# A macaron encoder layer on one core: four matmuls on a cleared tile first, the first squares on VectorE, wide operand copies, loads by SyncE alone

## The chip, the cores and the metric

The kernel runs on one core of one Trainium2 chip. The metric is device time of one execution in microseconds. Before the change three runs gave 1293.13, 1294.99 and 1297.63 us, median 1294.99.

Engines go by the names of the profile: PE is TensorE (PEld its weight loads), DVE is VectorE, ACT is ScalarE, POOL is GpSimd, SP is SyncE, which here only issues transfers.

## The reference

One layer on 512 tokens of width 1024, all in float32:

```python
x = x + 0.5 * swiglu(rmsnorm(x, ffn1_norm), ffn1_w1, ffn1_w3, ffn1_w2)
h = rmsnorm(x, mix_norm)
x = x + hybrid_mixer(h, w_in, ...)      # dilated window attention | GQA | gates
x = x + 0.5 * swiglu(rmsnorm(x, ffn2_norm), ffn2_w1, ffn2_w3, ffn2_w2)
return rmsnorm(x, final_norm)

def rmsnorm(x, g):
    return x * lax.rsqrt(jnp.mean(x * x, axis=-1, keepdims=True) + EPS) * g
def swiglu(x, w1, w3, w2):
    return (jax.nn.silu(x @ w1) * (x @ w3)) @ w2
```

The feed-forward width is 2816, so w1 and w3 are each 22 chunks of 128 features. Only the opening of the first feed-forward part, and the start of the second, matter below.

## The kernel before

**Layout.** x lies transposed in eight tiles x0 to x7 of 128 features by 512 tokens. Every matmul of weights is done in three: each operand is split into a high part (H, a cast by ACT) and a low remainder (L, a subtraction by DVE), and H·H, L·H and H·L are added in PSUM (`mm3`, lines 223 to 225). So a block of 128 features needs hH and hL of each x tile (`norm_h`: x times the norm's gain) and wh and wl of the weights (`prep`, lines 208 and 209).

**The norm's factor is applied after the products.** They are made with x times gain; the factor per token, r = (mean of squares + eps)^-0.5, is multiplied into the result (`done1`, line 441: t = mm x R). It is made beside the first matmuls. `squares` lets ACT square each x tile, and `norm_sq` adds them into acc: on POOL for x1 to x5, on DVE for x6 and x7. `stat_r` sums acc over features with small matmuls (stat, line 383); DVE makes ms (line 375), POOL raises it to -0.5 (r, line 376). `stat_R` lets PE transpose r into all partitions (rb, line 391), and ACT copies that to R (line 393).

**The first feed-forward part** begins with four plain feature pairs. The first pair (`pair`) runs both its chunks side by side, tile by tile, as x and the weights land: 16 steps, numbered 0 to 15, each with three matmuls. Then six single chunks (`feat`) of eight steps follow. A table of hooks names the step behind which something is put into PE's order: squares at 12, stat_r at 23, stat_R at 27. PE's order is as written; the other engines' orders are set by a planner when the program is built, each engine then runs its own list strictly in that order.

From the fifth feature pair on the chunks are done by a Strassen scheme. It needs sums and differences of halves of the scaled x (TH, TL). `t_steps` prepares them in 15 steps of ACT and DVE, every second step from 12 on: `put` copies x times gain into raw tiles T (line 313), `sub` and `neg` form the combinations (lines 326, 327), `part` splits them (lines 318, 319). The second feed-forward part does the same from step 1 on, at every step.

**Buffers and queues.** Weights land in three buffers wr of 512 KB each; three pairs of wh and wl take their split forms, so a cast waits until PE is done with the chunk three before. The Strassen weights come in wa and wt: SP loads wt (line 189), then POOL issues a transfer that adds a second matrix onto it (line 190); DVE adds wt and wa into ws (line 207). Four PSUM banks hold products: a fifth chunk starts when the first product is multiplied by R. x tiles 1 and 3 are issued by ACT's queue, all others and the weights by SP's.

Of the kernel before, what the change touches and what calls it, by code (L numbers as in the profile page):

```python
# [11 lines left out]
F32 = mybir.dt.float32  # L12
# [18 lines left out]
GAP_B = 1  # L31
LAG = 1
LAST = 2
T = 512
D = 1024
NK = 8
# [32 lines left out]
class Layer:  # L69
    def __init__(self, ctx, tc, a):  # L70
        self.tc, self.nc, self.a = tc, tc.nc, a
        ctx.enter_context(tc.manual_schedule(engines={mybir.EngineType.PE}))
        pool = lambda n, **k: ctx.enter_context(tc.tile_pool(name=n, **k))
        self.dram = pool("dram", bufs=1, space=DRAM)
        self.cst = pool("cst", bufs=1)
        self.wb = pool("wb", bufs=1)
        self.tmp = pool("tmp", bufs=4)
        self.psm = pool("psm", bufs=4, space=PSUM)
        self.psa = pool("psa", bufs=4, space=PSUM)
        nc = self.nc  # L80
        c = self.cst
        self.x = [c.tile([128, T], F32, name=f"x{d}") for d in range(NK)]
        self.par = c.tile([128, 48], F32, name="par")
        nc.scalar.dma_start(self.par, a["par"])
        self.ident = c.tile([128, 128], F32, name="ident")
        self.ones = c.tile([128, 1], F32, name="ones")
        nc.vector.memset(self.ones, 1.0)
        self.mhalf = c.tile([128, 4], F32, name="mhalf")
        nc.vector.memset(self.mhalf, -0.5)
        nc.scalar.activation(self.ones, self.ones, AF.Copy)  # L90
        self.r = c.tile([128, 8], F32, name="r")
        self.R = c.tile([128, T], F32, name="R")
        self.acc = c.tile([128, T], F32, name="acc")
        self.open_h()
        self.gate_d = self.dram.tile([16, 128, T], F32, name="gate_d")
        self.qk_d = self.dram.tile([2 * NSQ, 128, T], F32, name="qk_d")
        self.items = ([("v", 0), ("v", 1), ("sw", 0), ("v", 2)] + [("g", j) for j in range(2)]
                      + [("qk", f) for f in range(NSQ, 12)] + [("g", j) for j in range(2, 9)]
                      + [("b", g) for g in range(3)] + [("g", j) for j in range(9, 16)])
        span = {"v": ("wav", 4), "qk": ("waq", 2), "g": ("wg", 1), "b": ("wb", 4)}  # L100
        self.order = self.ffn_order("a")
        for kind, n in self.items:
            if kind == "sw":
                self.order += [("swq", at) for at in self.slots(range(0, NSQ, 2))]
                continue
            name, m = span[kind]
            self.order += [(name, m * n + i) for i in range(m)]
        self.order += [("wab", i) for i in range(12)] + [("wo", i) for i in range(8)]
        self.order += self.ffn_order("b")
        self.raws, self.tiles, self.used, self.wx, self.TQ = {}, [], 0, None, None  # L110
        self.rings = {k: [] for k in BUFS}
        self.index = {it[:2]: n for n, it in enumerate(self.order)}
        self.kind = [self.home(it) for it in self.order]
        self.todo = sorted((n for n, t in enumerate(self.kind) if t != "ws"), key=lambda n: n - EARLY * (self.kind[n] == "wt"))
# [187 lines left out]

    def t_steps(self, g, gp):
        nc = self.nc
        raw = []
        flat = lambda t, c: t[:, c].rearrange("p k n -> p (k n)")

        def put(d):
            if d == 0:
                both = [gp.tile([128, 2048], F32, tag=f"g{2 + c}", name=f"T{c}") for c in range(2)]  # L310
                raw.extend(both[c // 2][:, 1024 * (c % 2):1024 * (c % 2) + 1024] for c in range(4))
            for half in range(2):
                nc.scalar.activation(raw[(0 if d < 4 else 2) + half][:, 256 * (d % 4):256 * (d % 4) + 256],
                                     self.x[d][:, 256 * half:256 * half + 256], AF.Copy, scale=self.par[:, g + d:g + d + 1])

        def part(c):
            src, H, L = raw[c], flat(self.TH, max(0, c - 1)), flat(self.TL, max(0, c - 1))
            nc.scalar.copy(H, src)
            nc.vector.tensor_sub(L, src, f32(H))

        def part1(k):
            src, H, L = raw[1][:, 256 * k:256 * k + 256], self.hH[k][:, 256:512], self.hL[k][:, 256:512]
            nc.scalar.copy(H, src)
            nc.vector.tensor_sub(L, src, f32(H))

        sub = lambda o, a, b: nc.vector.tensor_sub(raw[o], raw[a], raw[b])
        neg = lambda o, a, b: nc.vector.scalar_tensor_tensor(raw[o], raw[a], -1.0, raw[b], op0=ALU.mult, op1=ALU.subtract)
        return ([lambda d=d: put(d) for d in range(NK)]
                + [lambda: sub(0, 0, 1), lambda: sub(1, 3, 1), lambda: neg(3, 3, 0), lambda: part(0),
                   lambda: neg(2, 3, 2), lambda: part(3), lambda: part(2)], [lambda k=k: part1(k) for k in range(4)])  # L330
# [27 lines left out]
        nc.scalar.activation(self.hH[d], self.x[d], AF.Copy, scale=gc)  # L358
        nc.vector.scalar_tensor_tensor(self.hL[d], self.x[d], gc, f32(self.hH[d]), op0=ALU.mult, op1=ALU.subtract)

    def norm_sq(self, d):
        nc = self.nc
        if d == 0:
            nc.scalar.activation(self.acc, self.x[d], AF.Square)
        else:
            sq = self.tmp.tile([128, T], F32, tag="t", name="sq")
            nc.scalar.activation(sq, self.x[d], AF.Square)
            eng = nc.vector if d >= NK - 2 else nc.gpsimd
            eng.tensor_add(self.acc, self.acc, sq)

    def rpow(self, dst, src, inv):
# [713 lines left out]
    def layer(self, out):  # L1085
        nc, tc = self.nc, self.tc
        for n in range(2):
            self.raws[n] = self.ring("wr", self.todo.pop(0), 0, n)
            self.tiles.append(self.ring("wh", n, 0, n))
        for d in (1, 3):  # L1090
            nc.scalar.dma_start(self.x[d], self.a["x"][d])
        for d in range(NK):
            if d not in (1, 3):
                nc.sync.dma_start(self.x[d], self.a["x"][d])
            if d % 2 == 0:
                s = slice(128 * d, 128 * d + 256)
                for c in range(2):
                    nc.sync.dma_start(self.raws[c][:, s], self.a["w13a"][c][:, s])
            self.norm_h(d, G_FFN1)
            if d % 2 == 0:  # L1100
                for raw, (H, L) in zip(self.raws.values(), self.tiles):
                    nc.scalar.copy(H[:, s], raw[:, s])  # L1102
                    nc.vector.tensor_sub(L[:, s], raw[:, s], f32(H)[:, s])
        nc.sync.dma_start(self.ident, self.a["ident"])

        def squares():
            for d in range(NK):
                self.norm_sq(d)

        with tc.tile_pool(name="bt", bufs=1, side="right") as bp:  # L1110
            hooks = {12: squares, 23: self.stat_r, 27: self.stat_R, "T": (12, 2)}
            self.bias_open(bp)
            side = {(0, d): lambda g=d: self.bias_rows(g) for d in range(3)}
            for h in range(8):
# [101 lines left out]
```

## Time and profile before

| what | us |
|---|---|
| median of three runs | 1294.99 |
| the profiled execution | 1294.96 |
| its span, first to last instruction | 1293.2 |
| PE busy | 1269.7 |
| first matmul | 5.89 |
| longest idle time of PE behind the first matmul | 3.47, at the transposes rb |
| ACT, DVE, POOL busy | 589.5, 880.8, 125.9 |

Times in the profile count from the span's start. A timeline row gives start, duration, engine, source line, operation, output<-input and shape, and in brackets the idle time of that engine just before with what ended it; several equal instructions in a row are merged with their count. Matmuls overlap, so the step between two starts is what one costs. The granted clock of the whole execution is 0.994 of full speed.

### The profile page before, as it was taken

Reading aid. Unit: us, or ns where it says so; the run is one execution under the profiler, and the core shown is the slowest. Engines: PE = TensorE matmul, PEld = TensorE weight load, DVE = VectorE, ACT = ScalarE, POOL = GpSimd, SP = SyncE. Lnnn points to the kernel's source line nnn. Section 1 sums busy time; section 2 is a strip of 40 time slices with the busy share of each in tenths; the row PEclk is TensorE's granted clock in tenths of the full one; section 3 lists DMA queues with packets and bytes.
Section 4 is the critical chain, followed back from the end, with each engine's and each line's share of the span. In section 5 each row is a group of like instructions: output and inputs, shape, how many; then the busy total and the mean of one; then the engine's idle time right before and its main releaser. Section 6 shows DMA issues by size and latency. Waiting matters only on the chain.

```text
span 1293.2 us, 19954 instructions
## 1 busy us (share of the span) xinstructions
PE 1269.7 (98%) x7994; PEld 1124.1 (87%) x7994; DVE 880.8 (68%) x1334; ACT 589.5 (46%) x883; POOL 125.9 (10%) x128
## 2 busy tenths in 40 slices
PE   7999999999999999999999999999999999999997
PEld 5897899899889999877888878888889989988996
DVE  5775578558783687576657898655577847774775
ACT  7552355235463443545324455543475415442553
POOL 3111011010110112100001100000301000100001
PEclk9999999999999999999999999999999999999998
DMA  8664776351373774743232221345627636753322
GB/s 255 195 175 155 205 179 175 131 135 48 123 205 122 205 196 155 246 108 92 98 112 81 75 74 41 106 151 165 214 83 193 182 94 175 170 165 98 99 82 66
DMA packets 85549, 181.91 MB, mean 141 GB/s; under 512 B 12480, under 2 KB 19024, under 8 KB 85456
## 3 DMA queue, kind: packets, MB, share of 16 engines
q1 hardware_dynamic: 67616, 140.22, 32.5%
q0 software_dynamic: 16832, 39.34, 15.1%
q8 instruction: 63, 1.03, 0.3%
q10 hardware_dynamic: 1008, 1.07, 0.2%
q14 instruction: 30, 0.25, 0.1%
HBM read 168.98 MB, written 15.29 MB: 142 GB/s over the span
## 4 chain that ended last, share of the span: by engine, by line
PE 87%; DVE 4%; DMA 4%; issue 3%; POOL 1%; ACT 1%; SPq 0%; POOLq 0%; DVEq 0%
PE mm L223 23%; PE mm L225 22%; PE mm L224 22%; PE Y L223 3%; PE Y L224 3%; PE Y L225 3%; DMA wt<-in_waq 2%; PE X L223 2%; PE X L225 2%; PE X L224 1%; PE S L776 1%; DVE wl L209 1%; PE mm L827 1%; PE Tb L966 1%; PE T L845 1%
## 5 line engine op out<-in xcount | busy, mean ns | idle before, releaser
L208 ACT CAST wh<-wr 128x1024 fp32r<-128x1024 f32 x142 | 148.8, 1049 | 216.1 <-PE mm L224 137.9
L209 DVE TENSOR_TENSOR wl<-wr,wh 128x1024 fp32r<-128x1024 f32 x142 | 173.5, 1223 | 58.4 <-ACT wh L208 58.0
L223 PE MATMUL mm<-hH,wh 128*128 128x256 f32 (+1 forms) x600 | 201.9, 336 | 5.9 <-ACT wh L1102 5.9
L225 PE MATMUL mm<-hH,wl 128*128 128x256 f32 (+1 forms) x600 | 198.1, 330 | 0.0
L224 PE MATMUL mm<-hL,wh 128*128 128x256 f32 (+1 forms) x600 | 197.7, 330 | 0.0
L223 PE MATMUL mm<-gg,wh 128*128 128x512 f32 (+1 forms) x376 | 143.1, 380 | 0.0
L225 PE MATMUL mm<-gg,wl 128*128 128x512 f32 (+1 forms) x376 | 142.6, 379 | 0.0
L224 PE MATMUL mm<-gg,wh 128*128 128x512 f32 (+1 forms) x376 | 142.5, 379 | 0.0
L223 PEld LDWEIGHTS mm<-hH,wh 128*128 128x128 f32 x600 | 114.1, 190 | 19.8 <-ACT wh L1102 5.9
L225 PEld LDWEIGHTS mm<-hH,wl 128*128 128x128 f32 x600 | 113.8, 190 | 11.4 <-DVE wl L209 0.3
L224 PEld LDWEIGHTS mm<-hL,wh 128*128 128x128 f32 x600 | 113.8, 190 | 9.9
L208 ACT CAST wh<-wa 128x1024 fp32r<-128x1024 f32 x48 | 50.4, 1051 | 101.0 <-PE mm L224 49.4
L490 DVE TENSOR_TENSOR u<-mm,R 128x512 f32<-128x512 f32 (+1 forms) x52 | 33.8, 650 | 85.1 <-PE mm L225 84.9
L223 PE MATMUL mm<-TH,wh 128*128 128x256 f32 x304 | 84.8, 279 | 1.6 <-DVE c L462 1.6
L225 PE MATMUL mm<-TH,wl 128*128 128x256 f32 x304 | 84.7, 279 | 0.0
L224 PE MATMUL mm<-TL,wh 128*128 128x256 f32 x304 | 84.7, 278 | 0.0
L223 PEld LDWEIGHTS mm<-gg,wh 128*128 128x128 f32 x376 | 70.8, 188 | 15.2 <-issue 1.1
L225 PEld LDWEIGHTS mm<-gg,wl 128*128 128x128 f32 x376 | 70.8, 188 | 14.1
L224 PEld LDWEIGHTS mm<-gg,wh 128*128 128x128 f32 x376 | 70.9, 188 | 13.9
L208 ACT CAST wh<-ws 128x1024 fp32r<-128x1024 f32 x48 | 50.4, 1051 | 69.2 <-PE mm L224 51.3
L209 DVE TENSOR_TENSOR wl<-wt,wh 128x1024 fp32r<-128x1024 f32 x48 | 58.7, 1223 | 33.1 <-ACT wh L208 32.8
L208 ACT CAST wh<-wt 128x1024 fp32r<-128x1024 f32 x48 | 50.3, 1050 | 67.0 <-PE mm L224 37.2
(230 smaller groups left out, 3182.6 us busy)
## 6 DMA issues: line engine op xcount, KB each, us to landing
wr<-in_w2a SPq DMA_DIRECT2D x22, 512.0 KB, 3.3
wr<-in_w2b SPq DMA_DIRECT2D x22, 512.0 KB, 3.5
wt<-in_w13b SPq DMA_DIRECT2D x20, 512.0 KB, 3.6
wa<-in_w13b SPq DMA_DIRECT2D x20, 512.0 KB, 4.5
wt<-in_w13b POOLq DMA_DIRECT2D x20, 512.0 KB, 5.8
wt<-in_w13a SPq DMA_DIRECT2D x18, 512.0 KB, 3.4
wa<-in_w13a SPq DMA_DIRECT2D x18, 512.0 KB, 4.5
wt<-in_w13a POOLq DMA_DIRECT2D x18, 512.0 KB, 6.0
```

The lines of the kernel that those rows point to most:

```text
L208: self.nc.scalar.copy(H, raw)
L209: self.nc.vector.tensor_sub(L, raw, f32(H))
L223: mm(out, lH, rH, start=start, stop=False, skip_group_check=more)
L224: mm(out, lH, rL, start=False, stop=False, skip_group_check=more)
L225: mm(out, lL, rH, start=False, stop=stop, skip_group_check=more)
L490: nc.vector.tensor_mul(u, ps, R)
L776: nc.tensor.matmul(*args, start=True, stop=True)
L827: nc.tensor.matmul(oc, v, p, start=st, stop=sp)
L845: nc.tensor.transpose(ps[:, 128 * b:128 * b + 128], P[h][:, c0 + 128 * b:c0 + 128 * b + 128], self.ident)
L966: nc.tensor.transpose(pt[:, 128 * j:128 * j + 128], P[h, j][:, 128 * k:128 * k + 128], self.ident)
```

## The change

Five edits, all in the opening but the third:

1. POOL clears the tile R with a memset at the start, and PE multiplies it with itself four times (float32, 128 columns of weights, 256 moving) into a spare PSUM tile that nobody reads, ahead of everything else on PE.
2. In the first feed-forward part all seven additions of squares go to DVE (`norm_sq(d, 0)`); elsewhere POOL keeps its five.
3. `put` writes both halves of an x tile with one instruction of 512 columns, so `t_steps` has 8 copies in place of 16, in both feed-forward parts.
4. All eight x tiles are issued by SP, each ahead of the weights of its pair.
5. The hook of stat_R moves from step 27 to 28, and the T steps begin at 16 in place of 12.

```diff
+WARM = 4
@@ __init__
         self.R = c.tile([128, T], F32, name="R")
+        nc.gpsimd.memset(self.R, 0.0)
@@ t_steps
-        raw = []
+        raw, both = [], []
...
-                both = [gp.tile([128, 2048], F32, tag=f"g{2 + c}", name=f"T{c}") for c in range(2)]
+                both.extend(gp.tile([128, 2048], F32, tag=f"g{2 + c}", name=f"T{c}") for c in range(2))
                 raw.extend(both[c // 2][:, 1024 * (c % 2):1024 * (c % 2) + 1024] for c in range(4))
-            for half in range(2):
-                nc.scalar.activation(raw[(0 if d < 4 else 2) + half][:, 256 * (d % 4):256 * (d % 4) + 256],
-                                     self.x[d][:, 256 * half:256 * half + 256], AF.Copy, scale=self.par[:, g + d:g + d + 1])
+            nc.scalar.activation(both[d // 4].rearrange("p (a c) -> p a c", a=2)[:, :, 256 * (d % 4):256 * (d % 4) + 256],
+                                 self.x[d].rearrange("p (a n) -> p a n", a=2), AF.Copy, scale=self.par[:, g + d:g + d + 1])
@@ norm_sq
-    def norm_sq(self, d):
+    def norm_sq(self, d, pool=NK - 2):
...
-            eng = nc.vector if d >= NK - 2 else nc.gpsimd
+            eng = nc.vector if d >= pool else nc.gpsimd
@@ layer
-        for d in (1, 3):
-            nc.scalar.dma_start(self.x[d], self.a["x"][d])
+        warm = self.aux("warm")
+        for _ in range(WARM):
+            nc.tensor.matmul(warm[:, :256], self.R[:, :128], self.R[:, :256], start=True, stop=True)
         for d in range(NK):
-            if d not in (1, 3):
-                nc.sync.dma_start(self.x[d], self.a["x"][d])
+            nc.sync.dma_start(self.x[d], self.a["x"][d])
...
-                self.norm_sq(d)
+                self.norm_sq(d, 0)
...
-            hooks = {12: squares, 23: self.stat_r, 27: self.stat_R, "T": (12, 2)}
+            hooks = {12: squares, 23: self.stat_r, 28: self.stat_R, "T": (16, 2)}
```

The planner sets the order of POOL, DVE and ACT anew. Three places carry the prediction; line numbers of the changed kernel are one or two higher.

POOL, from the program's start to the first r, before:

```order
L1207 MEMSET const-uint8-127 128x1
L1211 UNCONDITIONAL_BRANCH
L369 ISA
L369 TENSOR_TENSOR acc<-acc,sq 128x512 x5
L190 DMA wt<-in_w13a 128x2x512
L376 TENSOR_TENSOR r<-ms,mhalf 128x4
L190 DMA wt<-in_w13a 128x2x512 x6
```

and in the change:

```order
L1208 MEMSET const-uint8-127 128x1
L1212 UNCONDITIONAL_BRANCH
L94 MEMSET R 128x512
L192 DMA wt<-in_w13a 128x2x512
L377 ISA
L377 TENSOR_TENSOR r<-ms,mhalf 128x4
L192 DMA wt<-in_w13a 128x2x512 x6
```

The five additions are gone; the ISA instruction, which stood at the front ahead of them, now stands behind the first wt transfer and just ahead of r.

DVE, from the low part of the last x tile (hL_111 before, hL_112 in the change) to the first product with R, before (T_274 and T_275 are the two raw tiles):

```order
L359 SCALAR_TENSOR_TENSOR hL_111<-x_81,par,hH_103 128x512
L209 TENSOR_TENSOR wl<-wr,wh 128x1024
L369 TENSOR_TENSOR acc<-acc,sq 128x512 x2
L209 TENSOR_TENSOR wl<-wr,wh 128x1024 x2
L326 TENSOR_TENSOR T_274<-T_274 128x1024
L207 TENSOR_TENSOR ws<-wt,wa 128x1024
L375 TENSOR_SCALAR ms<-stat 128x4
L209 TENSOR_TENSOR wl<-wr,wh 128x1024
L326 TENSOR_TENSOR T_274<-T_275,T_274 128x1024
L319 TENSOR_TENSOR TL<-T_274,TH 128x1024
L441 TENSOR_TENSOR t_375<-mm,R 128x512
```

and in the change (T_311 and T_312 are the raw tiles):

```order
L360 SCALAR_TENSOR_TENSOR hL_112<-x_81,par,hH_104 128x512
L370 TENSOR_TENSOR acc<-acc,sq 128x512 x3
L211 TENSOR_TENSOR wl<-wr,wh 128x1024
L370 TENSOR_TENSOR acc<-acc,sq 128x512
L327 TENSOR_TENSOR T_311<-T_311 128x1024
L211 TENSOR_TENSOR wl<-wr,wh 128x1024 x2
L327 TENSOR_TENSOR T_311<-T_312,T_311 128x1024
L376 TENSOR_SCALAR ms<-stat 128x4
L328 SCALAR_TENSOR_TENSOR T_312<-T_312,T_311 128x1024
L211 TENSOR_TENSOR wl<-wr,wh 128x1024
L320 TENSOR_TENSOR TL<-T_311,TH 128x1024
L328 SCALAR_TENSOR_TENSOR T_312<-T_312 128x1024
```

Three additions now stand ahead of the first wide wl; ws has left the stretch ahead of ms; and four instructions stand between ms and the first product with R, which follows the last row shown.

ACT, from its first x tile on, before (x_74 is x0, x_75 is x1):

```order
L358 ACTIVATE hH_96<-x_74,par 128x512
L1102 CAST wh<-wr 128x256 x2
L358 ACTIVATE hH_97<-x_75,par 128x512
L358 ACTIVATE hH_98<-x_76,par 128x512
L1102 CAST wh<-wr 128x256 x2
```

and in the change:

```order
L359 ACTIVATE hH_97<-x_74,par 128x512
L1103 CAST wh<-wr 128x256
L365 ACTIVATE acc<-x_74 128x512
L1103 CAST wh<-wr 128x256
L314 ACTIVATE T_311<-x_74,par 128x2x256
L359 ACTIVATE hH_98<-x_75,par 128x512
L359 ACTIVATE hH_99<-x_76,par 128x512
L1103 CAST wh<-wr 128x256 x2
L368 ACTIVATE sq<-x_75 128x512
```

Squares are now spread between the tiles, and all eight stand ahead of the first wide cast, where before five did. On SP x1 goes out ahead of x2 and x3 ahead of x4, and the first wt follows the first wide wr, ahead of the second and third, where before it came behind them.

## The prediction

> **What bounds the kernel now.** I read the page's first part, then PE's timeline of the opening, then the timelines of the engines that PE waits for there.
>
> ```profile
> PE 1269.7 (98%) x7994; PEld 1124.1 (87%) x7994; DVE 880.8 (68%) x1334; ACT 589.5 (46%) x883; POOL 125.9 (10%) x128
> ```
>
> PE is busy nearly throughout, so a change in other engines' work pays only where PE stands still or runs at a lower clock. The change touches the first 60 us and the start of the second FFN. PE's timeline of the opening (start, duration, then idle time before and who ended it):
>
> ```profile
> 5.89 0.80 PE L223 MATMUL mm<-hH,wh 128*128 128x512 f32 x1 [5.89 <-ACT wh L1102]
> 10.75 0.63 PE L225 MATMUL mm<-hH,wl 128*128 128x512 f32 x1
> 11.17 0.45 PE L223 MATMUL mm<-hH,wh 128*128 128x512 f32 x1
> ...
> 19.96 0.19 PEld L225 LDWEIGHTS mm<-hH,wl 128*128 128x128 f32 x1 [0.28 <-DVE wl L209]
> 24.88 0.40 PE L225 MATMUL mm<-hH,wl 128*128 128x512 f32 x1
> 25.38 1.05 PE L383 MATMUL stat<-ones,acc 128*128 128x1 f32 x8
> 26.29 0.48 PE L223 MATMUL mm<-hH,wh 128*128 128x512 f32 x1
> ...
> 28.68 0.39 PE L224 MATMUL mm<-hL,wh 128*128 128x512 f32 x1
> 28.90 0.40 PE L225 MATMUL mm<-hH,wl 128*128 128x512 f32 x1
> 32.77 1.11 PE L391 MATMUL rb<-ident,r 128*128 128x128 f32 x4 [3.47 <-POOL r L376]
> 33.53 0.78 PE L223 MATMUL mm<-hH,wh 128*128 128x512 f32 x1
> ...
> 38.37 0.50 PE L225 MATMUL mm<-hH,wl 128*128 128x512 f32 x1
> 38.71 0.39 PE L223 MATMUL mm<-hH,wh 128*128 128x512 f32 x1
> ```
>
> Starts lie 0.43 apart up to 11.17 and 0.23 apart after it: PE begins at about half clock. It then stands still once, for 3.47 us, at the transposes (rb) that spread the norm factor r, and comes back at half clock: 12 matmuls from 33.53 to 38.71 take 5.18 us. In the 0.28 wait at 19.96 it catches up with the second set of weights (wl). Why r is late stands on POOL and DVE:
>
> ```profile
> 16.10 7.71 POOL L369 TENSOR_TENSOR acc<-acc,sq 128x512 f32<-128x512 f32 x5 [15.65 <-ACT sq L367]
> 23.75 1.36 POOL L190 DMA_DIRECT2D wt<-in_w13a  x1
> 30.77 1.94 POOL L376 TENSOR_TENSOR r<-ms,mhalf 128x4 f32<-128x4 f32 x1 [5.66 <-DVE ms L375]
> ```
>
> ```profile
> 18.55 1.35 DVE L209 TENSOR_TENSOR wl<-wr,wh 128x1024 fp32r<-128x1024 f32 x1 [2.27 <-ACT wh L208]
> 23.84 1.49 DVE L369 TENSOR_TENSOR acc<-acc,sq 128x512 f32<-128x512 f32 x2 [3.93 <-POOL acc L369]
> 25.24 2.35 DVE L209 TENSOR_TENSOR wl<-wr,wh 128x1024 fp32r<-128x1024 f32 x2
> 27.51 1.22 DVE L326 TENSOR_TENSOR T<-T 128x1024 f32<-128x1024 f32 x1
> 29.38 1.22 DVE L207 TENSOR_TENSOR ws<-wt,wa 128x1024 f32<-128x1024 f32 x1 [0.65 <-DMA wt<-in_w13a]
> 30.53 0.15 DVE L375 TENSOR_SCALAR ms<-stat 128x4 f32<-128x4 f32 x1
> ```
>
> POOL needs 7.71 us for five additions and holds up the sum of squares. The stat matmuls end at 26.3, but the tiny ms sits on DVE behind two wl, T and a ws, which waits for the wt whose accumulating DMA POOL could issue only at 23.75. So r comes at 32.7.
>
> **The change, part by part.**
>
> *The wait for r.* In the order of the changed kernel ws stands behind ms, and the squares no longer pass POOL. The new time of r follows from ACT, whose cadences are these rows (the step between two of a merged row is its length less one instruction, over the count less one):
>
> ```profile
> 3.79 0.72 ACT L358 ACTIVATE hH<-x,par 128x512 fp32r<-128x512 f32 x1 [1.12 <-DMA par<-in_par]
> 5.43 0.40 ACT L1102 CAST wh<-wr 128x256 fp32r<-128x256 f32 x1 [0.92 <-DMA wr<-in_w13a]
> ...
> 9.89 0.70 ACT L1102 CAST wh<-wr 128x256 fp32r<-128x256 f32 x2
> 10.49 1.33 ACT L358 ACTIVATE hH<-x,par 128x512 fp32r<-128x512 f32 x2
> ...
> 15.40 2.18 ACT L367 ACTIVATE sq<-x 128x512 f32<-128x512 f32 x4
> 17.49 1.03 ACT L208 CAST wh<-wr 128x1024 fp32r<-128x1024 f32 x1
> 18.43 1.15 ACT L367 ACTIVATE sq<-x 128x512 f32<-128x512 f32 x2
> 25.11 3.31 ACT L313 ACTIVATE T<-x,par 128x256 f32<-128x256 f32 x8
> ```
>
> Steps: hH 0.61, square 0.52, narrow cast 0.30, wide cast 0.94, half copy T 0.40. The wide T copy isn't in this trace. Its elements are those of hH, the same operation with the same scale: 0.61, with two half copies (0.80) as the upper bound and one (0.40) as the lower. Up to the first wide cast ACT now has 8 hH, 8 squares, 8 narrow casts and one T: 4.9 + 4.2 + 2.4 + 0.6 = 12.1 us. From 3.79 the cast runs 15.9 to 16.9 if no load is late. With the waits of before it ends as before, at 18.5. I take 17.6, between. DVE has six of the seven additions before wl; after hL of x7 three are left, 0.6 each (23.84 has two in 1.49 while POOL was finishing), and they end near 17 as well. So wl, 18.55 to 19.9 before, ends at about 18.9 (18.2 to 19.9): a gain of **1.0 us** (0 to 1.7).
>
> From there PE has 22 matmuls (5.0), stat (0.9) and, with the hook at 28 in place of 27, 15 in place of 12 matmuls (3.4): it reaches the transposes at 28.3. DVE's ms waits for the second T subtraction, which needs the last T copy: 17.6 + 7 x 0.61 + 2 x 0.94 = 23.8, and 1.2 on, 25.0. PE's stat ends at 24.9. ms 0.15, a handover of 0.1 and 1.94 on POOL give r at 27.2, so 1.1 us are to spare. Removed: the gap (28.90 + 0.23 to 32.77) **3.64**; the half-clock stretch, 5.18 less 12 x 0.229, **2.43**; half-clock transposes, by these rows of the second FFN, where they cost 0.36 in place of 0.76, **0.40**; the wait of stat for acc (25.11 to 25.38), **0.27**.
>
> ```profile
> 953.43 0.60 PE L391 MATMUL rb<-ident,r 128*128 128x128 f32 x4
> 953.79 0.48 PE L223 MATMUL mm<-hH,wh 128*128 128x512 f32 x1
> ```
>
> *What is late next.* The next feature needs a PSUM bank that the first product with R frees. DVE reaches that product at ms + neg 1.2 + wl 1.2 + TL 1.2 + neg 1.2 + 0.65 = 30.6 (up to 31.3 if the cast before wl is late); PE is there at 28.3 + 0.36 + 9 x 0.229 = 30.7. Cost **-0.3** (0 to -0.9).
>
> *POOL's own start.* The order shows an ISA without tiles ahead of POOL's first tensor operation; the built program calls it a reload of POOL's library. It was hidden in the 15.65 us before 16.10. Now it stands behind the wt DMA and ahead of r. That DMA waits for SP's wt, which now follows the first wide load at once:
>
> ```profile
> 10.63 4.53 SPq L177 DMA_DIRECT2D wr<-in_w13a  x3
> wt<-in_w13a SPq DMA_DIRECT2D x4, 512.0 KB, 6.1
> ```
>
> 11.1 + 6.1 = 17.2, plus POOL's 1.36: the reload starts at 18.6. r may start as late as 26.1, so 7.5 us of it are free. Its price is between 0 and 15.3 us. At 16.10 the add began at once when its square was there, so nothing is left for the first call; I take it as hidden. The Trainium skill, GPSIMD Engine Reference, section Instruction dispatch, says that the first call to a freshly loaded POOL kernel pays an IRAM load of about 6 us that no profile row shows. By that figure, as an estimate, the load would end at 24.6 and cost nothing if it begins with the reload. No row of this trace shows its length.
>
> *The four matmuls on R.* Unseen at this size. Nearest rows, at full clock:
>
> ```profile
> 109.76 0.81 PE L590 MATMUL bps<-onehot,rel_bias 32*8 32x383 f32 x2
> 110.49 0.50 PE L223 MATMUL mm<-gg,wh 128*128 128x512 f32 x1
> ```
>
> 0.73 for 383 columns gives 0.49 for 256, and 0.92 at half clock: 3.7 us for four. After POOL's memset of R (0.1 as for a tiny one, 1.5 as for an addition of this size) they run from about 1.5 to 5.5, when PE had nothing to do; first weights come at 5.83 or up to 0.9 earlier. If they bring full clock by 8 in place of 11.17, PE keeps pace with ACT's feed. If not, 12 slow matmuls from 5.0 on end the pair near 18.4, still ahead of wl. Worth 0 to 0.5; no term of its own, as wl decides.
>
> *Loads by SP alone.* SP has two issues more (0.43 each), ACT two fewer. The bytes are the same.
>
> ```profile
> q1 hardware_dynamic: 1048, 1.39, 102.5%
> ```
>
> From 6 to 10 us SP's queue alone moved 1.39 MB, with the DMA engines full, so one queue is enough; x1 and x3 no longer go ahead of the first weights. It is in the range of wl above.
>
> *The second FFN* gets the eight wide copies too. At the transposes there PE waits for nothing (the two rows of 953 carry no idle time), though ACT makes sixteen narrow copies just before; eight wide ones take 8 x 0.61 in place of 16 x 0.40, and hide behind the same matmuls. Cost nothing; without that cover 1.5 us would be gained or lost.
>
> Sum: 3.64 + 2.43 + 0.40 + 0.27 + 1.0 - 0.3 = 7.4 us, own range 5.8 to 8.4. The profiled execution took 1294.96 against a median of 1294.99, so no correction: **1287.5 us**, own range 1286.5 to 1289.2.
>
> **The rivals.**
>
> *The reload is long (slower).* At the row's bound, 15.3 us from 18.6, r comes at 36.1. PE reaches the transposes 3.3 us later than before with 0.69 us more work done, and the half-clock stretch comes back: 1297.6. It decides from 7.5 us on; from 12.7 us the gain is gone. For it: nothing in the trace bounds it lower. Against it: it needs the far half of that bound. Chance 0.06.
>
> *The library comes in only with the first call.* Then it starts when ms is there, at 25.1, whatever was idle before, and every us over 1.1 is a stall. With the middle of the row's bounds, 7.6 us, r comes at 34.8, PE is 2.0 us later at rb with 0.69 done ahead, and the rest of the stall's cost is back: 1294.96 + 1.3 = 1296, no change that can be told. Against it: the add at 16.10 began with its square. Chance 0.10. By the wording of the page named above (the first call pays) this is the rival that it speaks for, and with its 6 us the time would be 1295, as an estimate.
>
> *A second wait remains.* Wide casts of third and fourth weights are late by 1 to 3 us, since wt now goes ahead of their loads, or ACT's and DVE's added opening work puts wl back to 19.9; PE then waits 1 to 2 us for r or wl. A wait of that length need not lower the clock:
>
> ```profile
> 1142.53 0.36 PE L223 MATMUL mm<-TH,wh 128*128 128x256 f32 x1 [1.55 <-DVE c L462]
> 1142.72 0.28 PE L224 MATMUL mm<-TL,wh 128*128 128x256 f32 x1
> ```
>
> After 1.55 us of idle the step stays short. 1287.5 + 1.0 + 2 = 1290.5, and 1293 with a half-clock stretch. Chance 0.14.
>
> *Given back later,* at a transfer that keeps its own time however early PE is: 1294. Loads are issued when PE frees a buffer, which speaks against it. Chance 0.04.
>
> **How the numbers follow.** Forecast 0.66. The range 1284.5 to 1293.5 takes in the third rival and, below, 3 us for the spread of runs (1293.13 to 1297.63 before). Within 0.3% (1291.1 to 1298.9) a measurement of this kernel can't tell from no change. Faster: 0.66 and three quarters of 0.14, 0.77. Same: the rest of the third, the fourth, the second and most of the first, 0.19. Slower 0.04.
>
> **What would show it.** Right: no PE idle over 1 us before rb, steps of 0.23 from about 8 us on without a break, rb at 28 to 29, the product with R by 31, and the first matmul of the Strassen steps about 7.4 us earlier than before. Wrong: PE idle at rb ended by POOL r, with r long after ms (a reload) or ms itself after 26 (a late cast); a stall at wl past 19.9; or Strassen steps that start 7 us earlier with an end that isn't.

## The result and the profile after

| | kernel before | changed kernel |
|---|---|---|
| median of 13 executions, us | 1296.77 (1293.13 to 1300.63) | 1288.98 (1286.59 to 1292.76) |
| profiled execution, us | 1294.96, span 1293.2 | 1289.2, span 1287.4 |

The ratio is 0.9942, 95% interval 0.9926 to 0.9958: faster by 0.6%, or 7.8 us of the medians. The forecast was 1287.5 us with a range of 1284.5 to 1293.5. Two later comparisons gave 0.9968 (0.9956 to 0.9980) and 0.9938 (0.9924 to 0.9953), so the gain is 0.3 to 0.6%.

PE's timeline of the changed kernel (start, duration, instruction, then idle time before it and who ended it), the opening and one place much later:

```profile
1.31 3.77 PE L1093 MATMUL warm<-R 128*128 128x256 f32 x8 [1.31 <-POOL R L94]
4.84 0.53 PE L225 MATMUL mm<-hH,wh 128*128 128x512 f32 x1
...
7.52 0.51 PE L225 MATMUL mm<-hH,wh 128*128 128x512 f32 x1 [0.66 <-ACT hH L359]
...
8.31 0.50 PE L226 MATMUL mm<-hL,wh 128*128 128x512 f32 x1 [0.28 <-DVE hL L360]
...
19.43 0.50 PE L227 MATMUL mm<-hH,wl 128*128 128x512 f32 x1 [0.99 <-DVE wl L211]
...
24.59 0.95 PE L384 MATMUL stat<-ones,acc 128*128 128x1 f32 x8
...
28.93 0.60 PE L392 MATMUL rb<-ident,r 128*128 128x128 f32 x4
29.29 0.48 PE L225 MATMUL mm<-hH,wh 128*128 128x512 f32 x1
...
53.42 0.28 PE L225 MATMUL mm<-hH,wh 128*128 128x256 f32 x1
...
217.56 0.36 PE L225 MATMUL mm<-TH,wh 128*128 128x256 f32 x1 [1.81 <-DVE c L463]
```

The transposes (rb) start at 28.93 with nothing to wait for; before they stood at 32.77 behind 3.47 us of idle. The next matmul follows 0.36 later at full clock. The first matmul of the Strassen steps (128x256) stands at 53.42. Its row before:

```profile
60.69 0.28 PE L223 MATMUL mm<-hH,wh 128*128 128x256 f32 x1
```

So 7.27 us were won by then. At 217.56 a wait of 1.81 us that the kernel before did not have at this matmul takes a part back: the lead of the same PE matmuls over the kernel before is 7.5 us ahead of it and 5.4 behind it. The profiled executions end 5.8 us apart.

ACT and VectorE, then POOL, of the changed kernel at the steps that the forecast rests on:

```profile
15.02 1.66 ACT L368 ACTIVATE sq<-x 128x512 f32<-128x512 f32 x3
...
15.97 2.28 DVE L370 TENSOR_TENSOR acc<-acc,sq 128x512 f32<-128x512 f32 x3
18.16 1.22 DVE L211 TENSOR_TENSOR wl<-wr,wh 128x1024 fp32r<-128x1024 f32 x1
...
25.58 0.16 DVE L376 TENSOR_SCALAR ms<-stat 128x4 f32<-128x4 f32 x1 [0.50 <-PE stat L384]
...
30.25 1.29 DVE L442 TENSOR_TENSOR t<-mm,R 128x512 f32<-128x512 f32 x2
```

```profile
17.51 1.36 POOL L192 DMA_DIRECT2D wt<-in_w13a  x1 [16.25 <-DMA wt<-in_w13a]
25.82 1.94 POOL L377 TENSOR_TENSOR r<-ms,mhalf 128x4 f32<-128x4 f32 x1 [6.96 <-DVE ms L376]
```

ms follows stat at once, r follows ms at once, and r ends at 27.76, 1.2 us ahead of PE's arrival.

### The profile page after: what moved, and what is told of

Same layout as the page of the kernel before. It is cut to its first block, busy times and chain, and to the rows that moved or that the text cites. A ratio compares the mean times of both kernels' runs of the same rounds, so it can differ in the third digit from the quotient of the medians.

```text
span 1287.4 us, 19953 instructions
## 1 busy us (share of the span) xinstructions
PE 1269.0 (99%) x8002; PEld 1122.4 (87%) x8002; DVE 883.6 (69%) x1339; ACT 586.4 (46%) x867; POOL 119.2 (9%) x124
## 4 chain that ended last, share of the span: by engine, by line
PE 86%; DVE 6%; issue 3%; DMA 3%; ACT 1%; SPq 0%; POOL 0%; POOLq 0%; DVEq 0%; ACTq 0%
PE mm L225 23%; PE mm L227 22%; PE mm L226 22%; PE Y L226 3%; PE Y L227 3%; PE Y L225 3%; DVE wl L211 2%; PE X L225 1%; PE X L227 1%; PE X L226 1%; PE mm L828 1%; PE Tb L967 1%; PE S L777 1%; PE T L846 1%; DMA d<-SO 1%
```

## The experiments

Twelve kernels ran, in three groups on three chips; two of the twelve are the changed kernel again. All ratios are to the kernel before on the same chip. The medians of the kernel before were 1296.84, 1290.59 and 1294.08 us in the three groups, so ratios are compared, not times. Beside the time stands where rb and the first Strassen matmul are in the one profile of each kernel; the kernel before has a profile from one chip only. One row of the change's order turned out to matter most: the place of the first weight sum **ws<-wt,wa** in VectorE's list, which is worked off strictly in order.

| kernel | first ws stands ahead of | additions 1 to 5 | rb starts (idle before) | first Strassen matmul | ratio to before |
|---|---|---|---|---|---|
| before | ms | POOL | 32.77 (3.47) | 60.69 | 1 |
| squares only | ms | VectorE | 31.24 (2.67) | 58.04 | 1.0016 (0.9995 to 1.0037) |
| hooks and wide copies only | ms | POOL | 31.43 (1.68) | 57.76 | 1.0009 (1.0000 to 1.0017) |
| loads and squares | first product with R | VectorE | 28.68 (0) | 59.89 | 1.0019 (1.0007 to 1.0032) |
| loads only | nothing that PE waits for soon | POOL | 31.33 (0) | 56.51 | 0.9963 (0.9945 to 0.9981) |
| ws moved only | as above | POOL | 28.77 (0) | 54.50 | 0.9965 (0.9949 to 0.9980) |
| loads, squares, ws moved | as above | VectorE | 28.82 (0) | 56.01 | 0.9979 (0.9968 to 0.9991) |
| changed, squares on POOL | as above | POOL | 31.52 (0) | 56.30 | 0.9949 (0.9930 to 0.9968) |
| changed, no early matmuls | as above | VectorE | 28.98 (0) | 53.47 | 0.9960 (0.9942 to 0.9977) |
| changed | as above | VectorE | 28.93 (0) | 53.42 | 0.9942, 0.9968, 0.9938 |

The column on ws is read from the built programs' lists, the others from the runs. Every kernel with ws ahead of ms or of the product with R is no faster than before; every one with ws behind them is. The landmarks in the profiles are a weaker guide: the second and third kernels reach the Strassen steps 2.7 and 2.9 us earlier than before and still have no better median.

### The four matmuls ahead of the weights

The changed kernel without them and without the memset of R:

```diff
-        nc.gpsimd.memset(self.R, 0.0)
...
-        warm = self.aux("warm")
-        for _ in range(WARM):
-            nc.tensor.matmul(warm[:, :256], self.R[:, :128], self.R[:, :256], start=True, stop=True)
```

> The changed kernel without the four matmuls on R and without the memset of R; the orders of the other engines are the same. Theory (r arrives in time, so the matmuls ahead of the weights are spare): the clock rises only near 11.2 us again, PE's first pairs end near 18.4 in place of catching up with every operand, PE still meets wl at about 19, so the transposes (rb) start at 28.9 to 29.3 without a wait, and the time is 0 to 0.4 us over the changed kernel: about 6 us under the kernel before. Rival (the early clock itself carries a part of the gain): at half clock PE comes late to wl, loses up to 2.4 us (the price of the half-clock stretch before) and the time is about 3.4 us under the kernel before.

Measured: 1292.14 us median, ratio 0.9960 (0.9942 to 0.9977). PE's timeline:

```profile
19.49 0.50 PE L226 MATMUL mm<-hH,wl 128*128 128x512 f32 x1 [1.01 <-DVE wl L210]
...
28.98 0.60 PE L391 MATMUL rb<-ident,r 128*128 128x128 f32 x4
...
53.47 0.28 PE L224 MATMUL mm<-hH,wh 128*128 128x256 f32 x1
```

At wl, at rb and at the first Strassen matmul it is 0.05 or 0.06 us behind the changed kernel. PE's steps shorten from 0.43 to 0.23 only near 8 us, but it meets the same wait for wl, so the slow start costs nothing there. The theory holds for the opening. The median is 4.7 us under the kernel before, between the 6 of the theory and the 3.4 of the rival, and the ratio's interval overlaps that of the changed kernel, so the time alone would not decide. The profiled execution lost its time far from here (below, on the clock).

### Squares on POOL again, and the loads alone

The changed kernel with the additions of squares 1 to 5 back on POOL:

```diff
-                self.norm_sq(d, 0)
+                self.norm_sq(d)
```

> The changed kernel with the additions of squares 1 to 5 on POOL again; everything else as changed. Theory (r was late because a wt subtraction stood ahead of ms on VectorE and because its DMA was issued late, not because POOL adds slowly): acc is complete near 17.6, one wide subtraction (wl) ends near 20, ms near 26, r near 28.2, rb starts at about 29.5 without a long wait; at most 1 us over the changed kernel. Rival (POOL's additions are the cause of the stall, as the prediction's step 'squares no longer pass POOL' has it): acc late, ms near 30, a wait of 3 us or more before rb and half clock after it; 5 to 6 us over the changed kernel.

The kernel before with only the loads of x1 and x3 moved to SP:

```diff
-        for d in (1, 3):
-            nc.scalar.dma_start(self.x[d], self.a["x"][d])
         for d in range(NK):
-            if d not in (1, 3):
-                nc.sync.dma_start(self.x[d], self.a["x"][d])
+            nc.sync.dma_start(self.x[d], self.a["x"][d])
```

> The kernel before with only the loads of x1 and x3 moved to SP's queue. The planner then puts the squares earlier between the first products, and ws behind ms on VectorE. Theory (order on VectorE is what decides): the wait at rb goes or falls under 1 us and the half-clock stretch with it, about 5 to 6.5 us under the kernel before, with POOL's additions still there. Rival (each edit takes its own part of the gain, and the loads are worth only the 1 us of an earlier wl): 0 to 1.5 us under the kernel before, with over 2 us of wait left at rb.

Measured: 1291.17 us, 0.9949 (0.9930 to 0.9968), and 1294.08 us, 0.9963 (0.9945 to 0.9981). In both there is no wait at rb at all, so POOL's additions do not cause the stall, and the order on VectorE does away with it. But rb comes at 31.5 and 31.3, where the theory had 29.5 for the first, and the loads alone gain 2.8 us of the medians, between the 5 to 6.5 of the theory and the at most 1.5 of the rival. This is why rb is late, on VectorE and then on POOL of the first of the two:

```profile
11.76 1.85 DVE L1104 TENSOR_TENSOR wl<-wr,wh 128x256 fp32r<-128x256 f32 x2
13.54 3.47 DVE L360 SCALAR_TENSOR_TENSOR hL<-x,par,hH 128x512 fp32r<-128x512 f32 x2
16.93 1.83 DVE L1104 TENSOR_TENSOR wl<-wr,wh 128x256 fp32r<-128x256 f32 x2
```

```profile
9.33 1.30 POOL L370 TENSOR_TENSOR acc<-acc,sq 128x512 f32<-128x512 f32 x1 [8.07 <-ACT sq L368]
11.76 6.39 POOL L370 TENSOR_TENSOR acc<-acc,sq 128x512 f32<-128x512 f32 x4 [1.13 <-ACT sq L368]
```

The same two kinds of instruction in the changed kernel, where POOL adds nothing:

```profile
10.11 1.41 DVE L360 SCALAR_TENSOR_TENSOR hL<-x,par,hH 128x512 fp32r<-128x512 f32 x2
11.43 0.75 DVE L1104 TENSOR_TENSOR wl<-wr,wh 128x256 fp32r<-128x256 f32 x2
```

While POOL adds, two hL take 3.47 us in place of 1.41 and two wl 1.85 in place of 0.75. PE waits for them three times (0.46, 0.95, 0.91) and once more for the next wl (0.51). So with the early squares, moving the additions to VectorE is worth 2.6 us at rb (31.52 against 28.93): not since POOL is late with its sum, which it ends at 18.15, ahead of VectorE's first addition at 19.35, but since it slows VectorE's operands. The Trainium skill, Advanced Engine Details and Errata, section Mode Summary, says that VectorE's second port is shared with GpSimd and that the two block each other where VectorE runs in a two-port mode. Here instructions with two float32 inputs were slowed. In the time the 2.6 us do not show: 0.9949 with POOL's additions and 0.9942 without can't be told apart.

### The squares alone, and the hooks with the wide copies

The kernel before with only the additions moved to VectorE (`eng = nc.vector` for all squares of this stage):

> The kernel before with only the additions of squares 1 to 5 moved to VectorE. In its order the subtraction ws still stands ahead of ms on VectorE. Theory (the additions on POOL delay the wt DMA, that delays ws, ws delays ms): POOL is free, so wt lands about 2.4 us earlier, ws ends near 28, r near 30.5, the wait at rb falls from 3.47 to about 1.4 us and the half-clock stretch goes: about 5 us under the kernel before. Rival (ws ahead of ms is the cause whatever POOL does): less than 1 us gained, the wait stays over 3 us.

The kernel before with only the wide copies (as in the change) and the later hooks:

```diff
-            hooks = {12: squares, 23: self.stat_r, 27: self.stat_R, "T": (12, 2)}
+            hooks = {12: squares, 23: self.stat_r, 28: self.stat_R, "T": (16, 2)}
```

> The kernel before with only the wide copies and the later hooks (28 and 16). On VectorE ws still stands ahead of ms, and squares 1 to 5 are still added on POOL, so the wt DMA still waits until about 23.8. Theory (these two edits do not touch what makes r late): three more matmuls stand ahead of rb (0.69 us), the wait there is 2.5 to 3 us, the clock falls behind it in part or whole; 0 to 1.5 us under the kernel before. Rival (a shorter ACT queue brings ms forward): wait under 1.5 us and 4 us or more gained.

Measured: 1299.83 us, 1.0016 (0.9995 to 1.0037), and 1291.48 us, 1.0009 (1.0000 to 1.0017). VectorE of the first, then PE of the first:

```profile
27.85 1.23 DVE L207 TENSOR_TENSOR ws<-wt,wa 128x1024 f32<-128x1024 f32 x1 [2.86 <-DMA wt<-in_w13a]
29.00 0.15 DVE L375 TENSOR_SCALAR ms<-stat 128x4 f32<-128x4 f32 x1
```

```profile
31.24 0.86 PE L391 MATMUL rb<-ident,r 128*128 128x128 f32 x4 [2.67 <-POOL r L376]
31.75 0.78 PE L223 MATMUL mm<-hH,wh 128*128 128x512 f32 x1
```

With POOL free the wt DMA was issued at 20.75 in place of 23.75, and still ws stood for 2.86 us until the data landed, with ms behind it. A stall of 2.67 us is left, and the clock falls (0.78 for the matmul after it). My theory had 1.4 us and no lower clock, the rival a wait of over 3 us and less than 1 us gained. The rival is nearer: with ws ahead of ms, freeing POOL takes 0.8 of 3.47 us off the stall. The first Strassen matmul is 2.65 us earlier than before, but this execution gives the lead back behind it, at waits like 2.09 us at 1142.35: its last transposes start at 1285.73, those of the kernel before at 1285.84.

In the second kernel the wait at rb is 1.68 us rather than the 2.5 to 3 of the theory. In that execution ACT waited 0.36 us for the last narrow weights where before it waited 1.67, and all behind it ran some 1.3 us earlier (POOL's first addition at 14.79 against 16.10, ms at 29.18 against 30.53), which covers the difference. Behind rb PE waits 1.53 us more for the first product with R, and the clock stays full. Neither edit brings a gain in time that can be told.

### Loads and squares together, and with ws moved

The kernel before with both of those edits, without the other two:

> The kernel before with two of the edits together: all loads on SP's queue, and the additions of squares on VectorE. No matmuls ahead of the weights, narrow T copies, old hooks (27 and 12). Theory (the loads' edit gives the order in which ms is free of ws, the squares' edit keeps POOL from slowing VectorE; the rest is spare): stat ends near 25.5, r near 27.9, rb starts at 28.2 to 28.8 with no wait over 0.3 us, Strassen steps start 6.5 to 7.4 us earlier than before, time within 1 us of the changed kernel. Rival (wide copies or the later hook are needed as well): the wait at rb is back with 1 us or more, and the time is over 2 us above the changed kernel.

Measured: 1292.49 us, 1.0019 (1.0007 to 1.0032): slower than before. PE's timeline, then VectorE's:

```profile
28.68 0.60 PE L391 MATMUL rb<-ident,r 128*128 128x128 f32 x4
...
36.21 0.50 PE L223 MATMUL mm<-hH,wh 128*128 128x512 f32 x1 [4.16 <-DVE t L441]
```

```profile
33.20 1.23 DVE L207 TENSOR_TENSOR ws<-wt,wa 128x1024 f32<-128x1024 f32 x1 [2.48 <-DMA wa<-in_w13a]
34.34 1.22 DVE L327 SCALAR_TENSOR_TENSOR T<-T 128x1024 f32<-128x1024 f32 x1
35.48 0.68 DVE L441 TENSOR_TENSOR t<-mm,R 128x512 f32<-128x512 f32 x1
```

The wait at rb is gone as the theory had it, and the time is lost again 7 us later: the next feature needs the PSUM bank that the first product with R frees, and that product stands behind T, which stands behind ws, which waits for a transfer. My theory fell: two edits do not make the change. Its rival (the wide copies or the later hook are needed as well) had the time right, but it put the wait at rb, where none came, and it names a condition, not the cause. This shows in a kernel in which only ws is moved as well:

```diff
+        if n == self.kind.index("ws") and len(self.prods) <= 2:
+            return False
...
+            if n == self.kind.index("ws"):
+                with self.tc.issue_after(self.prods[2].ins):
+                    self.nc.vector.tensor_add(raw, a, b)
...
-            nc.vector.tensor_mul(t[1], ps, self.R)
+            self.prods.append(nc.vector.tensor_mul(t[1], ps, self.R))
```

(`prods` holds the products with R in the order written; `issue_after` puts the sum behind the third of them in VectorE's list and adds no semaphore.)

> The kernel before with all loads on SP's queue, the squares' additions on VectorE, and the first ws issued behind the third product with R: the earlier pair of edits plus only the move of ws. Theory (the 4.2 us wait for the product with R in the pair came from ws ahead of it): rb near 28.7 without a wait as in the pair; the product with R runs near 32.9 in place of 35.5, so PE waits 0.5 to 1.6 us there in place of 4.2 and keeps its clock; 4 to 6 us under the pair's 1.0019 of the kernel before, so 0.2 to 0.3% under it. Rival (narrow copies or the early hook make that wait): a wait of over 3 us stays and the time is no better than the pair's.

Measured: 1291.15 us, 0.9979 (0.9968 to 0.9991), 2.9 us under the kernel before where the pair alone was 1.9 over it.

```profile
28.82 0.60 PE L398 MATMUL rb<-ident,r 128*128 128x128 f32 x4
...
33.91 0.50 PE L230 MATMUL mm<-hH,wh 128*128 128x512 f32 x1 [1.73 <-DVE t L448]
```

The wait falls from 4.16 to 1.73 us, a little over the 0.5 to 1.6 expected. The rest is VectorE's own work: with narrow copies the planner puts three T steps and two TL between ms and the product, in the changed kernel two and one. The changed kernel without the early matmuls differs from this one by the wide copies, the later hooks and the exact place of ws; it has no wait there, and its first Strassen matmul comes 2.5 us earlier (53.47 against 56.01). That is where the copies and hooks earn their place.

### Only ws moved

The kernel before with the same lines for ws and nothing else: loads, squares, copies and hooks stay. In the built lists ws and one wl<-wa a little later stand further back on VectorE, and every other engine's list is the same.

> The kernel before with one thing moved: the first weight sum ws<-wt,wa is issued on VectorE behind the third product with R, in place of ahead of ms. Loads, squares, copies and hooks as before; PE, ACT and POOL keep their lists. Theory (the stall is VectorE's queue standing at ws until a transfer lands): ms follows the first T subtraction at 28.7 in place of 30.5, r ends near 30.8, rb starts near 30.9 in place of 32.8 with a wait of 1.4 to 1.8 us left, which is what POOL's late additions make; the Strassen steps start 1.9 us earlier, or up to 4.7 us where the half-clock stretch goes too. Rival (the wait at rb has another cause that only the loads on one queue remove): rb stays within 0.5 us of 32.8.

Measured: 1289.10 us, 0.9965 (0.9949 to 0.9980), where the changed kernel on this chip had 1286.08. VectorE, then PE:

```profile
25.91 1.22 DVE L333 TENSOR_TENSOR T<-T 128x1024 f32<-128x1024 f32 x1
27.05 0.16 DVE L382 TENSOR_SCALAR ms<-stat 128x4 f32<-128x4 f32 x1
```

```profile
28.77 0.60 PE L398 MATMUL rb<-ident,r 128*128 128x128 f32 x4
...
54.50 0.28 PE L230 MATMUL mm<-hH,wh 128*128 128x256 f32 x1
```

One sum moved in one list brings 4.98 of the 8.00 us that the whole change brings on this chip, and in the profile the stall is gone. I had expected 1.4 to 1.8 us of it to stay. In this execution VectorE's opening ran 1.6 us earlier than in the profile of before (this T at 25.91 against 27.51), and r took 1.04 us rather than 1.94, so that part of the clean start at rb is this execution's; the median is not.

### POOL's reload measured

The changed kernel with an addition of four columns as POOL's first tensor operation. In its list the reload stands directly ahead of that addition.

```diff
+        nc.gpsimd.tensor_tensor(self.r[:, 0:4], self.mhalf, self.mhalf, op=ALU.add)
```

> The changed kernel with a four-column addition on POOL as its first tensor operation, on values that are there at 0.9 us; its result is not used. POOL's library reload then stands ahead of it with nothing else to hide behind. It measures the reload: the start of this addition less about 1.3 us (end of the memset of R) is its length. Theory (hidden in the changed kernel, where r began 6.95 us after the end of the wt DMA): at most 6.95 us, and no change of the time (within 1 us of the changed kernel). Rival (the library is loaded at the first call or is longer): over 7 us, or r itself comes earlier after ms than the 0.1 us handover of the changed kernel and the time falls by more than 1 us.

POOL's timeline:

```profile
0.74 0.52 POOL L94 MEMSET R<- 128x512 f32 x1 [0.29 <-POOLq L1209]
1.31 0.20 POOL L96 TENSOR_TENSOR r<-mhalf 128x4 f32<-128x4 f32 x1
```

The addition begins 0.05 us after the memset ends and takes 0.20. So in this program neither the reload nor the first call shows any time worth naming, and the ratio, 0.9970 (0.9959 to 0.9980), is that of the changed kernel in the same group (0.9968). The 6 us that the Trainium skill, GPSIMD Engine Reference, section Instruction dispatch, gives for a first call are not seen in this program.

### The later sums

Two controls of the changed kernel ran, one in each of the last two groups.

> The changed kernel itself once more, to stand beside its variants on the same chip. Both theories: about 8 us under the kernel before, as in the first comparison (1288.98 against 1296.77); the waits in the opening at the same places; the waits for c at the weight sums made with the accumulating wt transfer may fall at other places in the program, since they depend on when a transfer lands.

> The changed kernel once more, as the mark for the last variant on this chip. Every theory: faster than the kernel before by 0.3 to 0.6%, as in the two comparisons so far (0.9942 and 0.9968); a wait of 1 to 2 us for c at one to three of the Strassen groups.

They gave 1285.39 and 1286.08 us, 5.2 and 8.0 us under the kernel before on their chips; 8 had been expected of the first. Their waits for c fall at other places than in the first profile: neither waits near 217, one waits 1.30 us at 1012.52 and 0.52 at 1134.18, the other 1.66 at 1133.88. Beside the second ran the changed kernel with seven later sums of the kind ws<-wt,wa put behind an eviction of a Strassen group (S4); the planner shifted a few evictions on VectorE and four casts on ACT around them:

```diff
+            back = 1 if name[2] == "q" else 2
+            if key[1] == "S2" and len(self.s4) >= back:
+                with self.tc.issue_after(self.s4[-back].ins):
+                    self.nc.vector.tensor_add(raw, a, b)
...
```

> The changed kernel with seven later sums ws<-wt,wa issued four to six instructions later on VectorE (behind an eviction that was ready anyway); the opening is the same. In the changed kernel VectorE stood idle for 2 to 5 us at these sums until their transfer landed, and PE waited 1.81 us near 217 and 1.41 near 1136 for c behind them. Theory (the same queue wait as in the opening gave a part of the gain back): these waits for c fall under 0.5 us each, the time is 1 to 3 us under the changed kernel. Rival (the sums are needed as early as they stand, or VectorE's backlog has another source): the waits stay or appear at the sums' own matmuls, no change or 1 to 3 us over it.

Measured: 1283.14 us (1282.52 to 1283.55), 0.9911 (0.9897 to 0.9925): 2.9 us under the changed kernel on the same chip, and clear of its fastest execution (1285.94). One of the seven places in the control, VectorE and then PE:

```profile
1117.54 1.22 DVE L209 TENSOR_TENSOR ws<-wt,wa 128x1024 f32<-128x1024 f32 x1 [3.62 <-issue]
1118.68 0.68 DVE L463 TENSOR_TENSOR c<-mm,c 128x512 f32<-128x512 f32 x1
```

```profile
1133.88 0.35 PE L225 MATMUL mm<-TH,wh 128*128 128x256 f32 x1 [1.66 <-DVE c L463]
```

and the same place with the sum moved:

```profile
1113.34 0.68 DVE L469 TENSOR_TENSOR c<-mm,c 128x512 f32<-128x512 f32 x1
...
1118.18 0.69 DVE L471 TENSOR_TENSOR c<-Y,c 128x512 f32<-128x512 f32 x1 [0.53 <-PE Y L233]
1118.79 1.22 DVE L213 TENSOR_TENSOR ws<-wt,wa 128x1024 f32<-128x1024 f32 x1
```

In the control VectorE stands still for 3.62 us at the sum although the eviction behind it is ready. The view names no releaser for this wait (issue), but POOL issued the adding transfer at 1111.79 and it landed 5.7 us later, when the sum starts. VectorE then works off the backlog for 16 us and is late for PE by 1.66. With the sum behind the eviction the idle time is filled with work, and PE has no wait for c over 0.25 us in the whole execution. The theory holds at its upper end, and this version beats both kernels.

## Why the prediction was right, point by point

**The stall, the half-clock stretch, the transposes, stat's wait (3.64 + 2.43 + 0.40 + 0.27).** All four are gone as written, so the mechanism was right here. Predicted against measured: ms 25.0 and 25.58, r's end 27.2 and 27.76, time to spare 1.1 and 1.2, rb 28.3 and 28.93.

**wl earlier by 1.0 (0 to 1.7).** Mis-sized: PE's matmul behind wl moved from 19.96 to 19.43, 0.53. The wide cast ended at 17.6 as taken, but the three additions that I had ending near 17 ended at 18.2, and wl stands behind them. They began late, at 15.97, and each took 0.80 in place of the 0.6 that I had counted, by the same rule for merged rows (2.28 for three). Their squares were there in time: the last ended at 16.68, and the last addition began at 17.55. The pair of before already had this step (1.49 for two), which I had put down to POOL. Each addition reads the sum that the one before wrote, while two products with R, which don't, take a step of 0.61; that this dependence makes the difference is not shown. That half microsecond runs through ms, r and rb.

**The bank wait, -0.3.** It did not come: the first product with R ran from 30.25 to 30.9 (its end had been put at 30.6, with PE there at 30.7), and PE, later by as much, needed the bank only at 31.45. The pair of edits without the wide copies shows what such a wait can cost, 4.16 us. With 7.27 us in place of 7.4 at the first Strassen matmul the two misses nearly cancel.

**The reload.** Taken as hidden; with nothing to hide behind it showed 0.05 us. Both rivals on it fall.

**The four matmuls, no term of their own.** Right: 0.05 us at rb. The wide copy took 0.61 a step, as taken from hH.

**Given back later, chance 0.04.** This is the step that failed: I wrote that loads are issued when PE frees a buffer, and that this speaks against it. The second half of the wt weights is added by a transfer that POOL issues after another has landed, and VectorE's list stands still at the sum that needs it. In the profiled execution 1.81 us went that way at 217.56, and of the 7.27 won before, 5.8 were left at the end, which is in part the last sign of being wrong that I had named. The kernel before pays at the same kind of place (1.55 at 1142.53, where the changed kernel still waits 1.41 at 1136.60), and the two controls wait at others, so it is more a tax on both that falls differently in each execution than a loss of this change. Moving the sums ends it.

**The number.** That 7.8 us of the medians lie so near the sum of 7.4 is in part luck: the profiled executions lie 5.8 apart, and the second comparison gave a ratio of 0.9968, about 4 us.

**What made the gain.** I gave it to two things at once, ws behind ms and the squares off POOL. The first is the one: moving ws alone is worth 5.0 of 8.0 us, the squares alone nothing that the time shows. What set the place of ws was the planner's answer to the loads, not any line that speaks of ws. The squares mattered at rb in a way I did not see, by the slowed VectorE.

## What to carry to other kernels

On an engine that works off its list in order, look for the instruction that waits for a transfer and ask what stands behind it: here one sum ahead of a tiny one cost 5 us, and seven others 2.9. When an edit pays, compare the orders that it brought before crediting its own work; of the edits here tried alone or in twos, only those that moved the sum out of PE's way paid. A landmark far ahead of the end shows such effects: the first Strassen matmul of the changed kernel lies at 53.42, 53.20 and 53.22 in three profiles, where executions of one kernel lie up to 11 us apart. But two openings ran 1.3 and 1.6 us earlier than that of before for no reason in their edits, and a lead there can be gone at the end, as with the squares alone.

## What the runs showed of the hardware that was not expected

**Idle of about half a window can drop the clock.** The changed kernel's time without the early matmuls varied from 1286.64 to 1296.56, and the profiled execution had 3.4 us at half clock near 568, behind a wait that every kernel has there. The windows view (PE busy with its count, the others, then the granted clock PEclk, DMA share and GB/s) of the kernel with only ws moved, then of the one with loads, squares and ws:

```profile
448.40:451.80 3.40, 1.62 (x12) 1.24 (x11) 3.40 (x5) 1.53 (x2) 0.00 (x0) 1.00 0.57 103
451.80:455.20 3.40, 3.40 (x19) 3.40 (x18) 3.37 (x5) 0.00 (x0) 0.00 (x0) 0.51 0.59 193
```

```profile
1137.20:1140.60 3.40, 1.48 (x13) 1.51 (x14) 3.40 (x5) 0.46 (x2) 0.00 (x0) 0.99 1.00 216
1140.60:1144.00 3.40, 3.40 (x17) 3.23 (x16) 3.00 (x4) 2.05 (x3) 0.00 (x0) 0.51 1.06 343
```

And of one and the same place of the program, in the changed kernel without the early matmuls and in the one with the squares alone:

```profile
564.35:567.76 3.41, 1.58 (x19) 1.27 (x19) 3.41 (x10) 0.59 (x1) 0.00 (x0) 1.00 0.31 91
567.76:571.17 3.41, 3.41 (x10) 2.63 (x9) 1.35 (x4) 0.41 (x1) 0.00 (x0) 0.50 0.15 62
```

```profile
567.43:570.84 3.41, 1.58 (x18) 1.25 (x18) 3.41 (x9) 0.59 (x1) 0.00 (x0) 1.00 0.08 8
570.84:574.25 3.41, 3.41 (x26) 2.60 (x20) 2.84 (x9) 0.66 (x1) 0.00 (x0) 1.00 0.42 145
```

Stretches of 3.4 us with PE busy for 1.62, 1.48 and 1.58 us (48%, 44% and 46%) are followed by one at half clock, but one more with 1.58 us is not, so busy time alone does not decide near the half. In all kept traces, up to the last few us of the program where PE has only small matmuls left, every fall followed a stretch with PE busy for 48% or less, and none followed one over half.

The stretches have a fixed grid. In these traces the granted clock keeps one value for 3.41, 6.83, 20.48, 440.3 or 1273.2 us, all whole multiples of 3.413. The 1.81 us wait at 217.56 in the changed kernel fell across two stretches of that grid, counted from the rise to full clock near 4.9; PE was busy for 2.59 and 2.42 us of them, and the wait cost no clock. So a wait of this size costs its own length in one execution and, as an estimate (half of 3.4 us), 1.7 us more in another, by where the stretches begin. The Trainium skill, TensorE: Matmul & The Clock Gate, section What's actually happening, has a free-running window of 3413 ns, and the trace agrees with that; it asks for an idle window to fall back, and here about half a window could be enough.

**It goes with much of the spread.** The fastest of the kernel before in the first group had 1292.67 us at a mean granted clock of 0.997, the slowest 1303.80 at 0.990; as an estimate, 0.007 of 1290 us is 9 of these 11.

What stays open: why the wide copies with the later hooks had a median no better than before on their chip, though their profile is 2.9 us ahead of the one profile of before at the first Strassen matmul; how much of a lead in the opening the later sums take back in other executions than the profiled ones; why an r on POOL took 1.04 us in one kernel and 1.9 to 2.0 in the others; and why VectorE's wide wl was hardly slowed beside POOL's additions in the kernel before (1.35 against 1.22 us) where the small ones more than doubled.
